# Attention probabilities: one tile for each head, normalised tiles copied by DMA into fp32r tiles, and the copies transposed

## The chip, the cores and the metric

The kernel runs on 1 core of one Trainium2 chip. The metric is the device time of one launch in microseconds. Three runs of the kernel before gave 1145.41, 1145.74 and 1146.05 us; the median, 1145.74 us, is the time before.

## The reference

One layer on 2048 tokens of 1024 channels, with 256 context tokens. All inputs are float32.

```python
h  = rms_norm(x)   * (1 + scale)   + shift      # scale, shift, gate from silu(c) @ w_ada + b_ada
hc = rms_norm(ctx) * (1 + scale_c) + shift_c
rq, rk, rv, rg, aq, ak, av, ag = project(h, w_in)   # one combined projection
# group A: bidirectional retention, 4 heads of 128, in chunks of 128 tokens
ret_x = group_norm(retention_fwd(rq, rk, rv) + retention_bwd(rq, rk, rv)) * gn_w * silu(rg)
# group B: windowed attention, 8 query heads of 64 over 2 key/value heads
def sink_softmax(logits, sink):
    m = maximum(max(logits, axis=-1), sink)
    p = exp(logits - m)
    return p / (sum(p, axis=-1) + exp(sink - m))
# for a block of 128 queries: 256 context keys and the block's own keys with both neighbour blocks (384)
p   = sink_softmax(concat([q @ k_ctx.T, where(valid, q @ k_window.T, -1e30)]), sink[head])
att = p[:, :256] @ v_ctx + p[:, 256:] @ v_window
x   = x + gate * (concat([ret_x, att * silu(ag)]) @ w_out)
out = rms_norm(x) * final_norm_w
```

## The kernel before

Up to about 680 us the kernel computes the modulated inputs, all projections (rq, rk, rv, rg, aq, ak, av, ag) and the retention states, and leaves them in DRAM scratch tensors. To keep float32's accuracy on TensorE each operand is split into a high part, rounded to the type fp32r, and a low part, the rest; a product is then three matmuls (high by high, high by low, low by high).

From there on it walks over the 16 blocks of 128 tokens, `b` = 0 to 15. A block has two half-steps, one for each key/value head `kv`, which serves four query heads. The string `STEPS[kv]` gives the order in which the pieces of a half-step are written down, and `FIRST` that of the very first half-step. The letters that matter here:

- `a0` to `a3` (`att_head`): the scores of one query head of the **next** half-step. Four matmuls fill a PSUM tile `S` (there is one such tile), a VectorE pass adds the mask, copies the scores into SBUF and takes the row maximum, a small VectorE operation makes the exponent's bias, and ScalarE takes the exponential of 640 scores and of one further column, the sink, and sums the row. At the first and last block 512 scores take the place of 640.
- `N0` to `N3` (`att_norm`): VectorE takes the reciprocal of the sum and GpSimd multiplies the head's row by it.
- `T0` to `T4` (`att_t`): TensorE transposes the probabilities of all four heads for one block of 128 keys into a PSUM tile `pt`; ScalarE rounds it to the high part, VectorE subtracts for the low part (tile `phl`, two buffers). The transposes of `T0` read all four heads, so they need the last `N`.
- `V0` to `V4` (`att_v`): the two matmuls of probabilities by values (PSUM tile `o`); `O` (`att_out`) brings the result to SBUF, gates it and splits it (`ma`).
- `o0` to `o7` (`piece`): three matmuls each of the output projection (PSUM tiles `pz`), on retention's part `mr` or attention's part `ma`. They depend on little and fill TensorE's queue between the others.
- `S`, `q`, `R`, `B`, `r`, `Y`, `U`: retention of the next block: scores, GpSimd's product `qd` of the queries with the decays (`q`, held behind the latest `N`), the matmuls `y` (`R`), the statistics, the normalisation of `sd` on ScalarE (`r`), its transposes `yt` and their gating `gr` with the split `mr` (`Y`), and the state update `st` on VectorE (`U`). `f` and `F`: final norm and store of the block before.

The probabilities of a half-step stand in one tile `p` of 128 x 4 x 641 float32 with two buffers; GpSimd writes the four sink columns into it. Loads and stores of this part are issued by one queue, SP's, in the order of the program: a load whose buffer is still in use holds up what stands behind it. A scheduler places the written operations on the engines by its own estimate of their times, so an engine's order is not exactly that of `STEPS`; each engine then works through its own list in order.

```python
PB[(b, kv)] = (C2["pool"].tile([P, 4, 641], F32, tag="pb", ...), ...)
pool.tensor_copy(PB[(b, kv)][0][:, :, n], sink8[:, 4 * kv : 4 * kv + 4])
pe.transpose(ppt[:, j], pb[:, j, kt * P : (kt + 1) * P], ident)
```

Elsewhere in the program, in the projection stage, four 128 x 512 tiles and one 128 x 256 tile of values are already copied from SBUF to SBUF by DMA into fp32r tiles (`vrx<-vt`, `vrc<-vtc`, line 539) and transposed there against the fp32r identity `identr` (line 546).

Of the kernel before, what the change touches and what calls it, by code (L numbers as in the profile page):

```python
# [39 lines left out]
def tile_hymba(  # L40
# [175 lines left out]
    def behind(i):  # L216
        return tc.issue_after(i.ins) if i else nullcontext()
# [516 lines left out]
    def att_head(b, kv, j):  # L734
# [8 lines left out]
        if j == 0:  # L743
            PB[(b, kv)] = (
                C2["pool"].tile([P, 4, 641], F32, tag="pb", name=f"p{b}_{kv}"),
                C2["pool"].tile([P, 3, 4], F32, tag="m4", name=f"m4{b}_{kv}"),
            )
            pool.tensor_copy(PB[(b, kv)][0][:, :, n], sink8[:, 4 * kv : 4 * kv + 4])
        pb, m4 = PB[(b, kv)]
        psc = pS.tile([P, 1024], F32, tag="S", name=f"S{b}_{h}")  # L750
        for hl in range(2):
# [5 lines left out]
        PE["S"] = i  # L757
        dve.tensor_tensor_reduce(  # L758
            out=pb[:, j, 0:n], in0=psc[:, o : o + n], in1=mk, op0=ALU.add, op1=ALU.max,
            scale=1.0, scalar=-3e38, accum_out=m4[:, 0, j : j + 1],  # L760
        )
        dve.tensor_scalar(  # L762
            m4[:, 1, j : j + 1], m4[:, 0, j : j + 1], -0.125, nsink[:, h : h + 1], op0=ALU.mult, op1=ALU.min
        )
        act.activation(  # L765
            pb[:, j, 0 : n + 1], pb[:, j, 0 : n + 1], AF.Exp, bias=m4[:, 1, j : j + 1], scale=0.125,
            accum_out=m4[:, 2, j : j + 1],
        )

    def att_norm(b, kv, j):  # L770
        n = len(window(b)[0]) * P + CTX
        pb, m4 = PB[(b, kv)]
        dve.reciprocal(m4[:, 2, j : j + 1], m4[:, 2, j : j + 1])  # L773
        PE["norm"] = pool.tensor_scalar(  # L774
            pb[:, j, 0:n], pb[:, j, 0:n], m4[:, 2, j : j + 1], 0.0, op0=ALU.mult, op1=ALU.add
        )

    BANKS = {"o": 1, "z": 2, "t": 3}
# [67 lines left out]
    def tables():  # L846
# [347 lines left out]
    pw = ctx.enter_context(tc.tile_pool(name="pw", bufs=1, space=PSUM, reuse_waits="tile"))  # L1194
    fw, vctx = C2["fw"], C2["vctx"]

    PO, PH = {}, {}

    def att_t(b, kv, kt):
        pb = PB[(b, kv)][0]  # L1200
        ppt = bank(f"pt{b}_{kv}_{kt}")
        for j in range(4):
            pe.transpose(ppt[:, j], pb[:, j, kt * P : (kt + 1) * P], ident)  # L1203
        phl = s2.tile([P, 2, 4, P], F32R, tag="phl", name=f"phl{b}_{kv}_{kt}", bufs=2)
        PE["phl"] = act.activation(phl[:, 0], ppt, AF.Copy)  # L1205
        PE["low"] = dve.tensor_tensor(phl[:, 1], ppt, phl[:, 0], op=ALU.subtract)  # L1206
        PH[kt] = phl
# [61 lines left out]
    def final_sum(b):  # L1269
        ss = s2.tile([P, 1], F32, tag="ss", name=f"ss{b}")  # L1270
        junk = s1.tile([P, D], F32, tag="junk", name=f"junk{b}", bufs=1)
        act.activation(junk, XB[b], AF.Square, scale=1.0 / 32, accum_out=ss)
# [7 lines left out]
    def last(b):  # L1280

        xb = XB[b]
        ss = s2.tile([P, 2], F32, tag="sl", name="sl")
        junk = s1.tile([P, D], F32, tag="junk", name="junkl", bufs=1)
        rz = s2.tile([P, 1], F32, tag="rz", name="rzl")
# [173 lines left out]
```

## Time and profile before

| | |
|---|---|
| median of 3 runs | 1145.74 us |
| the profiled execution | 1146.56 us, of which the span from first to last instruction 1144.8 us |
| mean granted TensorE clock | 0.995 |
| busy share of the span | TensorE 98%, VectorE 69%, ScalarE 41%, GpSimd 29% |

The profile of one execution lists, for every engine, instructions with their start and duration, and what ended the idle time before them. `PE` is TensorE's matmul unit, `PEld` its weight loads, which run beside the matmuls; `DVE` is VectorE, `ACT` ScalarE, `POOL` GpSimd, `SPq` the queue that issues DMAs. `L1203` is line 1203 of the program. In the projection stage and in the block loop the same profile can be asked for stretches (busy time of each engine between two times), for a timeline, for groups of instructions by line, for waits, and for the DMAs with the time from their issue to their landing. The block loop repeats itself almost exactly: the first transposes of block 6 start at 851.70 us, those of block 7 at 880.53 us, a period of 28.83 us.

### The profile page before, as it was taken

The numbers are of one execution on the slowest core, as the hardware profiler recorded it, in microseconds if no ns is written. First come the engines' busy times: TensorE is split into PE (matmuls) and PEld (weight loads), VectorE is DVE, ScalarE is ACT, GpSimd is POOL, SyncE is SP. The second block draws the span as 40 slices with busy tenths as digits, with TensorE's granted clock in tenths as the row PEclk, the third lists the DMA queues.
The fourth block names the chain that finished last, engine by engine and source line by source line (L and its number), as shares of the span: only waits on it lengthen the run. The fifth ranks groups of instructions, "written<-read, shape, count | busy, mean of one in ns | idle before, by whom it ended". The sixth has DMA issues, their size and how long they took to land.

```text
span 1144.8 us, 18064 instructions
## 1 busy us (share of the span) xinstructions
PE 1126.0 (98%) x6317; PEld 971.5 (85%) x6318; DVE 786.0 (69%) x1900; ACT 474.1 (41%) x1032; POOL 327.6 (29%) x459
## 2 busy tenths in 40 slices
PE   9999999999999999999999999999999999999997
PEld 5887879989888889998888877888888888888885
DVE  7973994665674555656566457777777777777774
ACT  4344512332443002322111156555555566666553
POOL 0000020100111100002014344555555555555553
PEclk9999999999999999999999999999999999999999
DMA  9948893374675533543356275444444444444310
GB/s 334 337 148 262 292 284 127 116 264 138 196 231 170 148 105 88 177 125 107 115 170 205 88 195 208 133 132 130 132 130 132 133 133 132 134 134 134 98 56 37
DMA packets 140113, 183.43 MB, mean 160 GB/s; under 512 B 11251, under 2 KB 103155, under 8 KB 139894
## 3 DMA queue, kind: packets, MB, share of 16 engines
q1 hardware_dynamic: 124948, 174.64, 48.6%
q10 hardware_dynamic: 15074, 7.64, 2.2%
q8 instruction: 50, 0.82, 0.3%
q14 instruction: 41, 0.34, 0.1%
HBM read 130.19 MB, written 50.86 MB: 158 GB/s over the span
## 4 chain that ended last, share of the span: by engine, by line
PE 81%; DVE 7%; issue 5%; ACT 3%; DMA 2%; POOL 1%; POOLq 0%; DVEq 0%; ACTq 0%
PE pz L1253 14%; PE rk L340 7%; PE rv L353 7%; PE ag L340 6%; PE o L1216 6%; PE pt L1203 5%; PE aq L340 5%; PE rg L340 4%; PE rq L340 4%; PE S L752 4%; PE S L756 2%; PE av L340 2%; PE ak L340 2%; PE u L469 2%; DVE wss L214 1%
## 5 line engine op out<-in xcount | busy, mean ns | idle before, releaser
L765 ACT ACTIVATE p<-p,m 128x641 f32<-128x641 f32 (+1 forms) x128 | 104.6, 817 | 60.3 <-DVE m L762 59.9
L774 POOL TENSOR_SCALAR p<-p,m 128x640 f32<-128x640 f32 (+1 forms) x128 | 101.8, 795 | 89.3 <-DVE m L773 82.5
L1205 ACT ACTIVATE phl<-pt 128x512 fp32r<-128x512 f32 x156 | 92.6, 595 | 78.3 <-PE pt L1203 76.3
L1206 DVE TENSOR_TENSOR phl<-pt,phl 128x512 fp32r<-128x512 f32 x156 | 106.3, 683 | 24.1 <-ACT phl L1205 23.4
L758 DVE CUSTOM_DVE_ANT_0 p<-S,msk 128x640 f32<-128x640 f32 (+1 forms) x128 | 102.4, 800 | 13.3 <-PE S L756 6.6
L1253 PE MATMUL pz<-wg1h,ma 128*128 128x512 f32 x256 | 106.1, 420 | 0.1
L1253 PE MATMUL pz<-wg0h,mr 128*128 128x512 f32 x256 | 103.6, 409 | 0.6 <-DVE mr L115 0.6
L1203 PE MATMUL pt<-ident,p 128*128 128x128 f32 x624 | 93.2, 272 | 0.6 <-DVE glast L1186 0.6
L1203 PEld LDWEIGHTS pt<-ident,p 128*128 128x128 f32 x624 | 75.2, 140 | 9.2 <-ACT first L833 0.8
L752 PE MATMUL S<-kwin,aq 128*128 128x384 f32 (+1 forms) x256 | 79.4, 332 | 0.6 <-DVE m L758 0.5
L445 ACT ACTIVATE vw<-v,wdec 128x128 fp32r<-128x128 f32 x128 | 43.7, 393 | 84.9 <-DVE v L458 84.9
L756 PE MATMUL S<-kctx,aq 128*128 128x256 f32 x256 | 71.1, 280 | 0.0
L1216 PE MATMUL o<-phl,vwin 128*128 128x512 f32 x184 | 62.2, 416 | 1.3 <-DVE phl L1206 0.8
L1253 PEld LDWEIGHTS pz<-wg0h,mr 128*128 128x128 f32 x256 | 48.1, 188 | 9.3 <-DVE mr L115 0.9
L1253 PEld LDWEIGHTS pz<-wg1h,ma 128*128 128x128 f32 x256 | 48.1, 188 | 7.9 <-POOL ma L1231 0.5
L752 PEld LDWEIGHTS S<-kwin,aq 128*128 128x128 f32 x256 | 48.0, 188 | 7.6 <-DVE m L758 2.3
L756 PEld LDWEIGHTS S<-kctx,aq 128*128 128x128 f32 x256 | 48.2, 188 | 5.2
L1253 PE MATMUL pz<-wg0l,mr 128*128 128x512 f32 x128 | 50.6, 395 | 0.0
L1253 PE MATMUL pz<-wg1l,ma 128*128 128x512 f32 x128 | 50.3, 393 | 0.0
L447 DVE SCALAR_TENSOR_TENSOR vw<-v,wdec,vw 128x128 fp32r<-128x128 f32 x128 | 40.6, 362 | 6.8 <-ACT vw L445 6.7
L1227 DVE TENSOR_TENSOR mf<-o,ob 64x256 f32<-64x256 f32 x64 | 26.7, 417 | 24.4 <-ACT ob L1224 23.7
L1216 PE MATMUL o<-phl,vctx 128*128 128x512 f32 x128 | 41.6, 404 | 0.2 <-DVE phl L1206 0.2
(425 smaller groups left out, 3001.7 us busy)
## 6 DMA issues: line engine op xcount, KB each, us to landing
wss<-in_wss SPq DMA_DIRECT2D x32, 512.0 KB, 6.6
qkv<-d_qkv SPq DMA_DIRECT2D x15, 768.0 KB, 4.8
aq<-d_aq SPq DMA_DIRECT2D x64, 128.0 KB, 3.9
xb<-in_xn SPq DMA_DIRECT2D x16, 512.0 KB, 3.8
out<-xb SPq DMA_DIRECT2D x31, 256.0 KB, 5.0
st<-d_st SPq DMA_DIRECT2D x15, 512.0 KB, 8.4
d_g<-g ACTq DMA_DIRECT2D x28, 256.0 KB, 2.9
x<-in_xt SPq DMA_DIRECT2D x12, 512.0 KB, 5.2
```

The costliest lines, as they stand in the source:

```text
L340: pe.matmul(ps, w[:, a, k, c0 : c0 + P], ht[b][:, k, :], start=(k == 0 and i == 0), stop=(k == NK - 1 and i == 2),)
L353: pe.matmul(ps, ht[a][:, k, t * P : (t + 1) * P], w[:, b, k, :], start=(k == 0 and i == 0), stop=(k == NK - 1 and i == 2),)
L752: i = pe.matmul(psc[:, o:512].rearrange("p (s t) -> p s t", t=P), AQ[b][:, h, :], C2["kwin"][:, kv, hl, ksel], start=(hl == 0), stop=(hl = ...
L756: pe.matmul(psc[:, 512:768], AQ[b][:, h, :], C2["kctx"][:, kv, hl], start=(hl == 0), stop=(hl == 1))
L758: dve.tensor_tensor_reduce(out=pb[:, j, 0:n], in0=psc[:, o : o + n], in1=mk, op0=ALU.add, op1=ALU.max, scale=1.0, scalar=-3e38, accum_out= ...
L765: act.activation(pb[:, j, 0 : n + 1], pb[:, j, 0 : n + 1], AF.Exp, bias=m4[:, 1, j : j + 1], scale=0.125, accum_out=m4[:, 2, j : j + 1],)
L774: PE["norm"] = pool.tensor_scalar(pb[:, j, 0:n], pb[:, j, 0:n], m4[:, 2, j : j + 1], 0.0, op0=ALU.mult, op1=ALU.add)
L1203: pe.transpose(ppt[:, j], pb[:, j, kt * P : (kt + 1) * P], ident)
L1205: PE["phl"] = act.activation(phl[:, 0], ppt, AF.Copy)
L1206: PE["low"] = dve.tensor_tensor(phl[:, 1], ppt, phl[:, 0], op=ALU.subtract)
L1216: pe.matmul(PO[kv], vt, PH[kt][:, hl], start=(kt == 0 and hl == 0), stop=(kt == nkt - 1 and hl == 1))
L1253: pe.matmul(PZ[n2], m[:, a, k % RH, :], WG[k // 4][c][:, k % 4, s], start=(k == 0 and i == 0), stop=(k == NK - 1 and i == 2),)
```

## The change

Each query head gets a tile of its own, 128 x 641 float32, from a tag with three buffers. The sink column is copied into it by VectorE, head by head, behind the pass that writes the scores, in place of GpSimd's one copy for four heads. After GpSimd has normalised a head, SP issues a DMA that copies its 128 x 640 probabilities from SBUF to SBUF into a tile `pr` of type fp32r with room for four heads (two buffers). The transposes read `pr` against `identr` and write the PSUM tile as fp32r. In `STEPS`, `o1` is moved ahead of `T0` in both half-steps.

Around it: the final norm's weights `fw` are loaded when the block loop's pools are opened, and not with the tables before; `glast`, the last gate's tile, takes a buffer of the tag `aq`, whose second buffer so far held the queries of block 1; the two scratch outputs `junk` are bf16.

```diff
 STEPS = (
-    "a0 o0 O T0 r0 o1 a1 N0 T1 r1 o2 V0 U a2 N1 T2 o3 Y V1 o4 a3 N2 T3 o5 V2 q o6 T4 N3 o7 V3 S f V4",
-    "a0 o0 O T0 o1 a1 N0 T1 R F0 F1 V0 a2 N1 T2 B V1 o2 a3 N2 T3 o3 V2 o4 T4 r2 N3 o5 V3 o6 V4 o7",
+    "a0 o0 O o1 T0 r0 a1 N0 T1 r1 o2 V0 U a2 N1 T2 o3 Y V1 o4 a3 N2 T3 o5 V2 q o6 T4 N3 o7 V3 S f V4",
+    "a0 o0 O o1 T0 a1 N0 T1 R F0 F1 V0 a2 N1 T2 B V1 o2 a3 N2 T3 o3 V2 o4 T4 r2 N3 o5 V3 o6 V4 o7",
 )
...
         if j == 0:
             PB[(b, kv)] = (
-                C2["pool"].tile([P, 4, 641], F32, tag="pb", name=f"p{b}_{kv}"),
+                C2["pool"].tile([P, 4, 640], F32R, tag="pr", name=f"pr{b}_{kv}"),
                 C2["pool"].tile([P, 3, 4], F32, tag="m4", name=f"m4{b}_{kv}"),
+                [C2["pool"].tile([P, 641], F32, tag="pb", name=f"p{b}_{kv}_{i}", bufs=3) for i in range(4)],
             )
-            pool.tensor_copy(PB[(b, kv)][0][:, :, n], sink8[:, 4 * kv : 4 * kv + 4])
...
-        dve.tensor_tensor_reduce(
-            out=pb[:, j, 0:n], in0=psc[:, o : o + n], in1=mk, op0=ALU.add, op1=ALU.max,
+        i = dve.tensor_tensor_reduce(
+            out=pb[:, 0:n], in0=psc[:, o : o + n], in1=mk, op0=ALU.add, op1=ALU.max,
             scale=1.0, scalar=-3e38, accum_out=m4[:, 0, j : j + 1],
         )
+        with behind(i):
+            dve.tensor_copy(pb[:, n : n + 1], sink8[:, h : h + 1])
...
         PE["norm"] = pool.tensor_scalar(
-            pb[:, j, 0:n], pb[:, j, 0:n], m4[:, 2, j : j + 1], 0.0, op0=ALU.mult, op1=ALU.add
+            pb[:, 0:n], pb[:, 0:n], m4[:, 2, j : j + 1], 0.0, op0=ALU.mult, op1=ALU.add
         )
+
+        nc.sync.dma_start(pr_[:, j, 0:n].bitcast(F32), pb[:, 0:n])
...
-        fw = new("fw", [P, D])
-        nc.sync.dma_start(fw, fnw)
...
-        new("glast", [P, 2, GT])
+        C2["glast"] = c2.tile([P, 2, GT], F32, tag="aq", name="glast")
...
-    fw, vctx = C2["fw"], C2["vctx"]
+    vctx = C2["vctx"]
+    fw = s2.tile([P, D], F32, name="fw", bufs=1)
+    nc.sync.dma_start(fw, fnw)
...
-            pe.transpose(ppt[:, j], pb[:, j, kt * P : (kt + 1) * P], ident)
+            pe.transpose(ppt[:, j].bitcast(F32R), pb[:, j, kt * P : (kt + 1) * P], identr)
```

How the engines' lists change is shown at three places. The first is TensorE's list in block 6, second half-step, from the scores `S_0` of the next half-step's first head on. `pt_1_0` are the transposes of `T0`, `pt_1_1` those of `T1`; x4 is four instructions, one for each head in turn. Before:

```order
L752 MATMUL S_0_8559<-kwin,aq_8204 128x384
L756 MATMUL S_0_8559<-kctx,aq_8204 128x256
L752 MATMUL S_0_8559<-kwin,aq_8204 128x384
L756 MATMUL S_0_8559<-kctx,aq_8204 128x256
L1253 MATMUL pz_0_8567<-wg0h,mr_8472 128x512
L1253 MATMUL pz_0_8567<-wg0l,mr_8472 128x512
L1253 MATMUL pz_0_8567<-wg0h,mr_8472 128x512
L1203 MATMUL pt_1_0_8580<-ident,p_1_8376 128x128 x4
L1253 MATMUL pz_0_8567<-wg0h,mr_8472 128x512
```

And now, from the last rows of the projection on:

```order
L1259 MATMUL pz_0_8725<-wg0h,mr_8623 128x512
L1209 MATMUL pt_1_0_8741<-identr,pr_1_8519 128x128 x3
L753 MATMUL S_1_8749<-kwin,aq_8336 128x384
L757 MATMUL S_1_8749<-kctx,aq_8336 128x256
L753 MATMUL S_1_8749<-kwin,aq_8336 128x384
L757 MATMUL S_1_8749<-kctx,aq_8336 128x256
L1209 MATMUL pt_1_1_8761<-identr,pr_1_8519 128x128 x3
L1209 MATMUL pt_1_0_8741<-identr,pr_1_8519 128x128
L1209 MATMUL pt_1_1_8761<-identr,pr_1_8519 128x128
L813 MATMUL y_8769<-st_8225,qd_8657 128x128
```

Six projection matmuls stand ahead of `T0` now and not three, and the fourth head's transpose stands behind the scores `S_1` and three transposes of `T1`. In the first half-step it is alike: six projection matmuls, three transposes, the scores of the second head, the fourth transpose, then `T1` without anything between.

The second is ScalarE's list in block 6, first half-step, from `ob` (the copy that `O` makes) on; `p` with `m` is the exponential of a head, `phl` the rounding of a group of transposes, `sd` retention's normalisation, four heads in two pairs. Before:

```order
L1224 ACTIVATE ob_1_8390<-o_1_8284 64x512
L1205 ACTIVATE phl_0_0_8403<-pt_0_0_8398 128x512
L765 ACTIVATE p_1_8376,m_1_8377<-p_1_8376,m_1_8377 128x641
L833 ACTIVATE sd_8162<-sd_8162,ra_8315 128x128 x2
L1205 ACTIVATE phl_0_1_8426<-pt_0_1_8421 128x512
```

And now:

```order
L1230 ACTIVATE ob_1_8537<-o_1_8422 64x512
L768 ACTIVATE p_1_0_8521,m_1_8520<-p_1_0_8521,m_1_8520 128x641
L1211 ACTIVATE phl_0_0_8553<-pt_0_0_8548 128x512
L839 ACTIVATE sd_8293<-sd_8293,ra_8455 128x128 x2
L1211 ACTIVATE phl_0_1_8575<-pt_0_1_8570 128x512
```

The exponential and the rounding of the first group have changed places; the second rounding still stands behind both and behind a pair of `sd`.

The third is SP's list where the block loop begins: `aq` are the queries of block 1, `gr`, `ga`, `xb` the gates and inputs of block 0. Before:

```order
L684 DMA vwin_6830<-d_v 128x256
L715 DMA aq_6503<-d_aq 32x8x128 x3
L701 DMA gr_6409<-d_g 128x512
L730 DMA ga_6411<-d_g 128x256
L731 DMA xb_6412<-in_xn 128x1024
```

And now:

```order
L782 DMA pr_1_6288<-p_1_2_6292 128x512
L715 DMA aq_6443<-d_aq 32x8x128 x2
L782 DMA pr_1_6288<-p_1_3_6293 128x512
L1201 DMA fw<-in_fnw 128x1024
L701 DMA gr_6431<-d_g 128x512
L730 DMA ga_6433<-d_g 128x256
L731 DMA xb_6434<-in_xn 128x1024
```

The loads of block 0 stand behind the copy of the last head of block 0 and behind `fw`; the other half of `aq` follows after the loads of block 1's `qkv` and `st`.

More of the change, by code (lines that the diff above doesn't have):

```diff
@@ L765, in att_head @@
         act.activation(
-            pb[:, j, 0 : n + 1], pb[:, j, 0 : n + 1], AF.Exp, bias=m4[:, 1, j : j + 1], scale=0.125,
+            pb[:, 0 : n + 1], pb[:, 0 : n + 1], AF.Exp, bias=m4[:, 1, j : j + 1], scale=0.125,
             accum_out=m4[:, 2, j : j + 1],
@@ L1270, in final_sum @@
         ss = s2.tile([P, 1], F32, tag="ss", name=f"ss{b}")
-        junk = s1.tile([P, D], F32, tag="junk", name=f"junk{b}", bufs=1)
+        junk = s1.tile([P, D], BF16, tag="junk", name=f"junk{b}", bufs=1)
         act.activation(junk, XB[b], AF.Square, scale=1.0 / 32, accum_out=ss)
@@ L1283, in last @@
         ss = s2.tile([P, 2], F32, tag="sl", name="sl")
-        junk = s1.tile([P, D], F32, tag="junk", name="junkl", bufs=1)
+        junk = s1.tile([P, D], BF16, tag="junk", name="junkl", bufs=1)
         rz = s2.tile([P, 1], F32, tag="rz", name="rzl")
```

6 lines of the change are left out of this document (4 added, 2 removed).

## The prediction

> **What bounds the kernel now.** I read the shares of the span first, then the chain that ended last, then the block loop by stretches, then TensorE's waits there.
>
> ```profile
> span 1144.8 us, 18064 instructions
> PE 1126.0 (98%) x6317; PEld 971.5 (85%) x6318; DVE 786.0 (69%) x1900; ACT 474.1 (41%) x1032; POOL 327.6 (29%) x459
> PE 81%; DVE 7%; issue 5%; ACT 3%; DMA 2%; POOL 1%; POOLq 0%; DVEq 0%; ACTq 0%
> 680.00:715.00 35.00, 32.00 (x187) 26.37 (x186) 24.38 (x72) 21.45 (x42) 13.39 (x20) 1.00 0.62 207
> 715.00:1100.00 385.00, 385.00 (x2359) 342.35 (x2357) 305.84 (x890) 229.34 (x468) 207.44 (x296) 1.00 0.43 127
> PE y L807 <- DVE m L773: 1.0, 1, 1.0
> ```
>
> The columns of the two stretches are length, then busy time of TensorE, its weight loads, VectorE, ScalarE and GpSimd, then clock, DMA share and GB/s. Between 715 and 1100 us TensorE is busy for 385.0 of 385.0 us: nothing holds it up, so any instruction made shorter there shortens the kernel, and any wait that arises lengthens it. The last row is its longest wait in the whole block loop, 1.0 us, in the loop's first blocks. VectorE is busy for 305.84 of 385 us (79%).
>
> **What the change removes: time of the transposes.** The groups of four, as float32 in the loop and as fp32r where the kernel has them already:
>
> ```profile
> L1203 PE MATMUL pt<-ident,p 128*128 128x128 f32 x624 | 93.2, 272 | 0.6 <-DVE glast L1186 0.6
> 851.70 0.60 PE L1203 MATMUL pt<-ident,p 128*128 128x128 f32 x4
> 852.05 0.48 PE L1253 MATMUL pz<-wg1h,ma 128*128 128x512 f32 x1
> 852.36 0.39 PE L1253 MATMUL pz<-wg1l,ma 128*128 128x512 f32 x1
> 551.17 0.45 PE L546 MATMUL pvx<-identr,vrx 128*128 128x128 f32 x4
> 551.76 0.40 PE L340 MATMUL aq<-h0l,w_aaq 128*128 128x512 f32 x1
> ```
>
> From the group's start to the second matmul behind it pass 0.66 us (852.36 - 851.70) in float32 and 0.59 us (551.76 - 551.17) in fp32r: 0.07 us a group. 624 transposes are 156 groups, so **-10.9 us** if nothing else moves. A block has ten groups: -0.70 us of its period.
>
> **What it adds: a hop by DMA between the last `N` and `T0`.** Block 6, second half-step, on GpSimd and TensorE:
>
> ```profile
> 858.99 0.62 POOL L111 TENSOR_SCALAR mr<-gr 128x512 fp32r<-128x512 f32 x1 [0.49 <-DVE gr L1239]
> 859.69 1.31 POOL L1242 TENSOR_TENSOR mr<-gr,mr 128x512 fp32r<-128x512 f32 x1
> 860.97 0.80 POOL L774 TENSOR_SCALAR p<-p,m 128x640 f32<-128x640 f32 x1
> 861.74 2.54 POOL L792 TENSOR_TENSOR qd<-qkv,decq 128x512 f32<-128x512 f32 x2
> 864.25 0.81 POOL L774 TENSOR_SCALAR p<-p,m 128x640 f32<-128x640 f32 x1
> 864.16 0.34 PE L752 MATMUL S<-kwin,aq 128*128 128x384 f32 x1
> 864.75 0.40 PE L1253 MATMUL pz<-wg0h,mr 128*128 128x512 f32 x1
> 864.98 0.39 PE L1253 MATMUL pz<-wg0l,mr 128*128 128x512 f32 x1
> 865.45 0.60 PE L1203 MATMUL pt<-ident,p 128*128 128x128 f32 x4
> ```
>
> `N3` ends at 864.25 + 0.81 = 865.06 and `T0` starts at 865.45: it has 0.39 us to spare. GpSimd gets to `N3` late because it runs `mr`, `N2` and `qd` in one piece behind `gr`. In the new list the fourth head's transpose comes behind three more projection matmuls (0.23 us each by 864.75 and 864.98: 0.70), three transposes (3 x 0.07 = 0.22), four score matmuls (864.16 to 864.75: 0.59, and 0.08 for the change behind transposes, 852.36 - 852.05 less 0.23), and three transposes of `T1` (0.22): 865.45 + 1.81 = 867.26. So the list leaves 2.2 us for the hop. What it takes:
>
> ```profile
> vrx<-vt SPq DMA_DIRECT2D x4, 256.0 KB, 2.3
> vrc<-vtc SPq DMA_DIRECT2D x1, 128.0 KB, 2.1
> DMA to landing us min/median/max: 2.3/2.3/2.6
> out<-xb SPq DMA_DIRECT2D x31, 256.0 KB, 5.0
> ```
>
> These copies of 128 rows from SBUF to SBUF take 2.1 us for 128 KB and 2.3 for 256 KB from issue to landing; at 0.1 us per 64 KB, 320 KB take **2.4 us** (estimate). The bounds are 2.1 and the stores' 5.0 us, which stand behind a 768 KB load; I take the near row, since nothing large is issued ahead of this head's copy. Landing: 865.06 + 2.4 + 0.05 for SP to start = 867.5, already 0.2 us late. Two things widen it.
>
> TensorE itself arrives earlier: the five groups of the first half-step are shorter, 5 x 0.07 = 0.35 us, of which I give back 0.1 (the transposes `yt` are now mixed with other matmuls): 867.0.
>
> And `N3` moves later, through the first half-step:
>
> ```profile
> 848.63 0.81 POOL L774 TENSOR_SCALAR p<-p,m 128x640 f32<-128x640 f32 x1 [0.37 <-DVE m L773]
> 851.00 0.40 PE L1253 MATMUL pz<-wg1h,ma 128*128 128x512 f32 x1
> 852.33 0.60 ACT L1205 ACTIVATE phl<-pt 128x512 fp32r<-128x512 f32 x1 [1.80 <-PE pt L1203]
> 852.83 0.83 ACT L765 ACTIVATE p<-p,m 128x641 f32<-128x641 f32 x1
> 853.66 0.86 ACT L833 ACTIVATE sd<-sd,ra 128x128 f32<-128x128 f32 x2
> 854.43 0.58 ACT L1205 ACTIVATE phl<-pt 128x512 fp32r<-128x512 f32 x1
> 855.65 1.13 DVE L841 SCALAR_TENSOR_TENSOR st<-st,gC,st 128x128 f32<-128x128 f32 x4
> 856.69 0.82 DVE L758 CUSTOM_DVE_ANT_0 p<-S,msk 128x640 f32<-128x640 f32 x1
> 858.22 0.68 DVE L1239 TENSOR_TENSOR gr<-yt,gr 128x512 f32<-128x512 f32 x1
> ```
>
> There the hop itself fits: `N3` ends at 849.44 and the fourth transpose comes at 851.00 + 6 x 0.23 + 0.22 + 0.67 = 853.3, 3.9 us later. But the first group is complete only then, and no longer at 852.05. ScalarE now does the exponential first (852.85 to 853.7), the first rounding (to 854.2, 0.5 from start to next start), the `sd` pair (0.77, by 853.66 and 854.43), and starts the second rounding at 854.95, 0.5 us later than before. VectorE's `st` update follows it, then the third head's pass, then `gr`: all 0.5 us later, and 0.1 more for the new sink copy in between. `gr` feeds `mr`, and with `N2` and `qd` behind it `N3` ends near 865.65. Copy landed: 865.65 + 2.45 = 868.1, TensorE there at 867.0: it **stands still for 1.1 us in each block**, and what is queued behind, `T1`'s last transpose and the twelve `y`, waits with it. In blocks 1 to 14: 14 x 1.1 = **+15.4 us**; the 0.1 above: **+1.4**.
>
> By the Trainium skill's page "DMA: Bandwidth & Descriptors", section "Anatomy of one DMA — SWDGE (gpsimd) path", a DMA costs about 2.0 us plus bytes at 436 GB/s; for 320 KB that is 2.75 us, an estimate of mine for copies that here come from SP and not from GpSimd. The rows of `vrx` and `vrc` lie below it (2.6 by the rule for 256 KB, 2.3 measured); by the rule the sum would be 14 x 0.35 = 4.9 us larger.
>
> **The sink columns.** GpSimd loses 32 copies, VectorE gets 128:
>
> ```profile
> L748 POOL COPY p<-sink 128x4 f32<-128x4 f32 x32 | 6.1, 194 | 2.2 <-PE pt L1203 2.2
> L762 DVE TENSOR_SCALAR m<-m,nsink 128x1 f32<-128x1 f32 x128 | 26.2, 205 | 0.3
> ```
>
> The neighbour of one column takes 0.205 us, part of it overlapped with the next instruction; between nothing and 0.2 I take 0.1 us, 0.8 us a block of VectorE's 28.83. VectorE's slack (21%) hides it except on the chain above, where it is counted. The three head buffers cost nothing while the copies land: a buffer is written again three heads later, and heads are some 3 us apart. The `junk` tiles keep their instructions.
>
> **Where the loop begins.** In the new list `fw` (512 KB) and all loads of block 0 stand on SP behind the copy of block 0's last head:
>
> ```profile
> 681.78 0.38 SPq L701 DMA_DIRECT2D gr<-d_g  x1
> 684.75 0.69 POOL L774 TENSOR_SCALAR p<-p,m 128x512 f32<-128x512 f32 x1 [2.94 <-DVE m L773]
> 690.47 0.50 PE L1253 MATMUL pz<-wg0h,mr 128*128 128x512 f32 x1 [0.56 <-DVE mr L115]
> gr<-d_g SPq DMA_DIRECT2D x16, 256.0 KB, 5.0
> ```
>
> That head is normalised at 685.44, so `gr` is issued at about 686.4 in place of 681.78 and lands, at its median of 5.0, at 691.4; gating and splitting (0.68 and 0.42) let the projection start at 692.5 in place of 690.47. TensorE has nothing else in its list there: 2.0 us. Block 1's scores come later too, the second half of its queries being behind the loads of blocks 0 and 1, so all of block 0's projection is used up before block 1's first transposes, and its four `S` then follow each other at VectorE's pace: 0.82 for a pass behind the 0.59 of its matmuls, some 0.5 us idle each: 2.0 us. **+4 us**, between 0 (loads land in time) and 8.
>
> **The sum**: -10.9 + 15.4 + 1.4 + 4 = +9.9 us on the profiled execution's own 1146.56 us (span 1144.8 and 1.8 around it), 1156.5. That execution was 0.8 above the median of 1145.74, against which I forecast **1155.6 us**; by its own bounds (a wait of 0.7 to 1.6 us a block, the beginning 2 to 6) 1148 to 1165.
>
> **The rivals.** (1) The hop is hidden: TensorE waits 0.2 us or less a block. For it: only 0.2 us is missing before the two shifts, and `vrc` lands in 2.1. Against it: TensorE's own gain of 0.35 is certain to come off the margin. Sum -10.9 + 2.8 + 1.4 + 2 = -4.7: 1141; with no wait at all 1136.
>
> (2) The first half-step waits as well. `xb`'s load waits on SP until the store of the same buffer lands, 5.0 us by the row above, and in the new list the copy of the third head stands behind that load. From the point where the landing passes the end of `N2`, that copy is issued late and queues behind 512 KB; I price it at 1 us more in each of 14 blocks: 1170. Against it: even `N3`, the head behind it, has 3.9 us there.
>
> (3) Gain and waits cancel: a wait of 0.4 us (5.6) with 1.4 and 4 against 10.9, 1146.
>
> (4) The transposes don't get faster in the loop, say because the weight loads beside them set the pace: the same waits less TensorE's earlier arrival, 0.75 x 14 + 1.4 + 4, +16: 1162.
>
> **Chances.** Forecast 0.52, rival 1 0.26, rival 2 0.11, rival 3 0.08, rival 4 0.03. 0.2% (2.3 us) is about what a measurement of this kernel can tell from no change. Faster 0.26, within it 0.08, slower 0.52 + 0.11 + 0.03 = 0.66. The range takes in most of rival 1 and the lower part of rival 2: 1138 to 1168.
>
> **What would show it.** Right: TensorE's busy time falls by about 10 us, and the waits list a new row of `pt` on the DMA of `pr`, 14 times near 1 us, always at a second half-step's first group; `gr` to `N3` starts 0.5 us later against the block's first scores; the projection at the loop's start begins near 692.5. Wrong: a `pt` row that waits under 0.3 us, or waits in the first half-step, or a copy that lands in under 2.2 or over 3 us.

## The result, and the profile after

The changed kernel takes **1180.69 us** (median of four runs, 1180.29 to 1181.46), the kernel before 1145.89 on the same chip: ratio 1.0304, 95% interval 1.0286 to 1.0322, 34.8 us slower. I had forecast 1155.6, with a range up to 1168. The direction was right, the size was not.

The page of the changed kernel, then its stretches (columns as in the prediction), then the longest waits of TensorE for the copies between 740 and 1120 us (total, times, longest):

```profile
span 1178.7 us, 18728 instructions
PE 22%; POOL 7%; DMA 6%; DVE 4%; issue 2%; ACT 1%; SPq 0%; POOLq 0%; DVEq 0%
L1209 PE MATMUL pt<-identr,pr 128*128 128x128 f32 x624 | 76.3, 241 | 22.2 <-DMA pr<-p 20.0
pr<-p SPq DMA_DIRECT2D x112, 320.0 KB, 3.2
```
```profile
680.00:715.00 35.00, 30.39 (x156) 23.81 (x154) 17.77 (x54) 15.23 (x28) 10.55 (x14) 0.90 0.75 250
715.00:740.00 25.00, 18.13 (x99) 15.36 (x99) 16.62 (x50) 11.66 (x25) 11.10 (x14) 0.80 0.39 135
740.00:1100.00 360.00, 341.96 (x2092) 296.12 (x2090) 281.09 (x896) 208.10 (x420) 180.63 (x240) 1.00 0.64 215
```
```profile
PE pt L1209 <- DMA pr<-p: 18.0, 18, 1.3
```

The chain that ended last was TensorE for 81% before. Now the profile follows it back to 678.6 us only, so its shares add up to less than half of the span; within it TensorE has about half, and GpSimd and the copies come next. In the loop TensorE is busy for 341.96 of 360 us, where it had been busy throughout. Between 715 and 740 us, where nothing was missing before, it works 18.13 of 25 us at a granted clock of 0.80.

Where the 34 us lie is read from one recurring point, the first scores (`a0`) of a block's first half-step:

| first scores of | before | after | behind by |
|---|---|---|---|
| block 2 | 735.08 | 750.53 | 15.5 |
| block 3 | 763.91 | 781.33 | 17.4 |
| block 13 | 1052.25 | 1081.67 | 29.4 |
| block 14 | 1081.08 | 1111.66 | 30.6 |
| block 15 | 1109.78 | 1143.35 | 33.6 |
| end of the span | 1144.8 | 1178.7 | 33.9 |

So 15.5 us are lost **before block 2**, about 1.2 us in each block after it, 3.0 us in block 14 alone. Beside the wait below, TensorE also waits for copies in three first half-steps between blocks 3 and 12, up to 0.35 us each time. (In the expectations below, "block 2's second half-step starts at 750.5" means the first row of this table; the point belongs to the first half-step, the name is a slip of mine.)

The wait in the loop is the one forecast. Block 6, second half-step of the changed kernel, on GpSimd, SP and TensorE:

```profile
883.58 2.54 POOL L798 TENSOR_TENSOR qd<-qkv,decq 128x512 f32<-128x512 f32 x2
886.10 0.80 POOL L778 TENSOR_SCALAR p<-p,m 128x640 f32<-128x640 f32 x1
```
```profile
886.93 0.50 SPq L782 DMA_DIRECT2D pr<-p  x1
887.48 1.74 SPq L715 DMA_DIRECT2D aq<-d_aq  x3
```
```profile
885.28 0.34 PE L753 MATMUL S<-kwin,aq 128*128 128x384 f32 x1
887.24 0.37 PE L1209 MATMUL pt<-identr,pr 128*128 128x128 f32 x3
888.11 0.37 PE L1209 MATMUL pt<-identr,pr 128*128 128x128 f32 x3
889.78 0.36 PE L1209 MATMUL pt<-identr,pr 128*128 128x128 f32 x2 [1.29 <-DMA pr<-p]
```

`N3` ends at 886.90, the copy is issued at once, and the fourth head's transpose starts at 889.78, **2.88 us** behind `N3`. TensorE had reached it at 888.3; from the transpose's start before the wait to its start after it pass 1.54 us in place of 0.07, so the wait costs 1.47.

At the beginning the block's fourth set of scores waits for VectorE, which has block 0's projection and final norm first:

```profile
712.87 0.69 DVE L1264 TENSOR_TENSOR xb<-pz,xb 128x512 f32<-128x512 f32 x1 [2.94 <-PE pz L1259]
717.13 1.41 DVE L1283 SCALAR_TENSOR_TENSOR xb<-xb,rz,fw 128x512 f32<-128x512 f32 x2 [2.20 <-DMA st<-d_st]
718.46 0.82 DVE L759 CUSTOM_DVE_ANT_0 p<-S,msk 128x640 f32<-128x640 f32 x1
```
```profile
719.43 0.66 PE L753 MATMUL S<-kwin,aq 128*128 128x384 f32 x1 [5.03 <-DVE p L764]
```

(The name `st` in the second row is the profile's attribution: the norm needs `rz`, which GpSimd ends at 717.10.) The pass at 718.46 empties the one tile `S`; until then TensorE stands for 5.03 us, and the matmul behind the stop takes 0.66 us in place of 0.34.

### The profile page after: what moved, and what is told of

Read it like the earlier page. It is cut to its first block, busy times and chain, and to the rows that moved or that the text cites. A ratio compares the mean times of both kernels' runs of the same rounds, so it can differ in the third digit from the quotient of the medians.

```text
span 1178.7 us, 18728 instructions
## 1 busy us (share of the span) xinstructions
PE 1132.1 (96%) x6317; PEld 966.0 (82%) x6318; DVE 796.4 (68%) x2028; ACT 476.7 (40%) x1032; POOL 323.3 (27%) x427
## 5 line engine op out<-in xcount | busy, mean ns | idle before, releaser
L1259 PE MATMUL pz<-wg0h,mr 128*128 128x512 f32 x256 | 100.3, 407 | 1.2 <-DVE mr L115 1.0
L1259 PE MATMUL pz<-wg1h,ma 128*128 128x512 f32 x256 | 100.1, 409 | 0.1
L1209 PEld LDWEIGHTS pt<-identr,pr 128*128 128x128 f32 x624 | 70.1, 141 | 34.5 <-DMA pr<-p 23.0
L1209 PE MATMUL pt<-identr,pr 128*128 128x128 f32 x624 | 76.3, 241 | 22.2 <-DMA pr<-p 20.0
L753 PE MATMUL S<-kwin,aq 128*128 128x384 f32 (+1 forms) x256 | 84.2, 349 | 8.0 <-DVE p L764 5.0
L1222 PE MATMUL o<-phl,vwin 128*128 128x512 f32 x184 | 70.7, 445 | 2.0 <-DVE phl L1212 1.5
L1222 PEld LDWEIGHTS o<-phl,vwin 128*128 128x128 f32 x184 | 33.0, 193 | 12.5 <-ACT phl L1211 4.5
```

The lines of the kernel that those rows point to most:

```text
L753: i = pe.matmul(psc[:, o:512].rearrange("p (s t) -> p s t", t=P), AQ[b][:, h, :], C2["kwin"][:, kv, hl, ksel], start=(hl == 0), stop=(hl = ...
L1209: pe.transpose(ppt[:, j].bitcast(F32R), pb[:, j, kt * P : (kt + 1) * P], identr)
L1222: pe.matmul(PO[kv], vt, PH[kt][:, hl], start=(kt == 0 and hl == 0), stop=(kt == nkt - 1 and hl == 1))
L1259: pe.matmul(PZ[n2], m[:, a, k % RH, :], WG[k // 4][c][:, k % 4, s], start=(k == 0 and i == 0), stop=(k == NK - 1 and i == 2),)
```

## The experiments

All runs in one table. "Block 2" is the start of its first scores; "a block" is the mean period from block 3 to block 13, from the same starts. The ratio is against the kernel before on the same chip; its median was 1145.6 to 1146.8 us.

| run | us | ratio (95%) | block 2 | a block |
|---|---|---|---|---|
| before | 1145.9 | | 735.1 | 28.83 |
| changed | 1180.7 | 1.0304 (1.0286-1.0322) | 750.5 | 30.03 |
| e1 | 1147.4 | 1.0009 (1.0000-1.0019) | 734.9 | 28.83 |
| e2 | 1178.9 | 1.0286 (1.0263-1.0310) | 751.7 | 30.10 |
| e3 | 1172.0 | 1.0225 (1.0203-1.0247) | 752.0 | 29.15 |
| e4 | 1140.9 | 0.9964 (0.9953-0.9975) | 735.1 | 28.40 |
| e5 | 1177.9 | 1.0288 (1.0266-1.0310) | 750.7 | 30.25 |
| e6 | 1233.8 | 1.0770 (1.0750-1.0790) | 752.0 | 33.97 |
| e7 | 1228.5 | 1.0715 (1.0697-1.0733) | 750.0 | 34.17 |
| e8 | 1180.8 | 1.0307 (1.0288-1.0326) | 756.8 | 29.94 |
| e9 | 1182.7 | 1.0314 (1.0291-1.0336) | 750.7 | 30.30 |
| e10 | 1154.4 | 1.0072 (1.0045-1.0099) | 752.1 | 28.42 |
| e11 | 1154.7 | 1.0072 (1.0053-1.0091) | 740.0 | 29.15 |
| e12 | 1178.3 | 1.0290 (1.0260-1.0321) | 751.2 | 30.25 |
| e13 | 1151.2 | 1.0044 (1.0031-1.0056) | 735.3 | 29.11 |
| e14 | 1168.9 | 1.0194 (1.0178-1.0209) | 741.6 | 30.08 |
| e15 | 1156.4 | 1.0086 (1.0072-1.0101) | 740.2 | 29.21 |
| e16 | 1152.2 | 1.0050 (1.0035-1.0064) | 740.8 | 29.04 |
| e17 | 1149.9 | 1.0024 (1.0012-1.0035) | 737.4 | 29.22 |
| e18 | 1137.5 | 0.9925 (0.9910-0.9939) | 736.0 | 28.10 |

The profiles differ ahead of the loop, too: block 0's first scores start between 668.5 and 674.9 us, so a few microseconds in the column "block 2" say nothing. From block 0's first scores to block 2's pass 64.6 us before, 80.6 in the changed kernel, 65.2 in e1, 77.4 in e2, 66.7 in e4, 76.4 in e5, 78.6 in e9, 80.4 in e10, 69.8 in e11 and in e14.

**Is the beginning lost to block 1's queries? (e1, e2)** In the trace the first scores of block 1 come at 701.7 us where they had come at 681.6 (the 688.8 of the expectation is its second head). Comparing the lists, I found an error of mine in the third list shown above: in the kernel before the three loads `aq` there are block 2's. Block 1's four stand earlier, ahead of `kwin`:

```
L715 DMA aq_6421<-d_aq 32x8x128 x4
L679 DMA kwin<-d_k 64x2x128 x4
L684 DMA vwin_6501<-d_v 128x256
L684 DMA vwin_6830<-d_v 128x256
L715 DMA aq_6503<-d_aq 32x8x128 x3
```

Since `glast` takes a buffer of `aq`, block 1's queries now wait for block 0's last scores. That looked like the cause.

```diff
 e1 (before)  -        new("glast", [P, 2, GT])
              +        C2["glast"] = c2.tile([P, 2, GT], F32, tag="aq", name="glast")
 e2 (changed) -        C2["glast"] = c2.tile([P, 2, GT], F32, tag="aq", name="glast")
              +    two tiles of tag "pb" take its place
```

> The kernel before with one part of the change alone: the last gate's tile takes a buffer of the tag of the queries. Theory Q (block 1's queries find no buffer until block 0's last scores are done, so block 1's first scores come some 12 us later and TensorE runs out of work): block 1's first scores move from 688.8 us to 700 or later, and the time rises by 9 to 16 us, to 1155-1162. Rival S (the loop's beginning is lost on SP's queue, behind the copies and the load of fw, neither of which is here): 1145-1149, first scores before 693 us.

> The changed kernel with the last gate in two of the three head buffers instead of a buffer of the queries; copies, fw and all else stay. Q: block 1's queries are loaded as early as before, the start of block 2's second half-step comes back from 750.5 us to 735-738, and the time falls by 12 to 15 us, to 1165-1169. S: SP's queue is as full as in the changed kernel, 1177-1181.

Theory Q falls. In e1 block 1's first scores come at 696.7, 15 us later than before, and the time rises by 1.0 us (between 0 and 2.2). e2 gives 1.8 us back, within its interval; it is the weaker test, since its gate holds two of the three head buffers at first. The next runs add the clearest: e4 keeps the late queries and loses nothing.

**What is the wait in the loop, and what do the copies cost in all? (e3, e4)**

```diff
 e3 - o5 V2 q o6 T4 N3 o7 V3
    + o5 V2 o6 T4 N3 q o7 V3
 e4 - pb[:, 0:n], pb[:, 0:n], m4[...]        (GpSimd, in place)
    - nc.sync.dma_start(pr_[:, j, 0:n].bitcast(F32), pb[:, 0:n])
    + pr_[:, j, 0:n], pb[:, 0:n], m4[...]    (GpSimd, rounded)
```

> The changed kernel with q written behind N3 in the first half-step: on GpSimd the product qd changes places with the fourth head's normalisation, and nothing else moves. Theory W (the wait at the second half-step's first transposes is the copy of a head that GpSimd normalises late): N3 ends 2.5 us earlier, the copy lands 1.0 us before TensorE gets there, the wait of 1.47 us a block goes: 14 x 1.47 = 20.6 less, 1160 (1157-1164). Rival L (the copy is held up by the loads and the third head's copy that were issued ahead of it, and lands at the same time whenever it is issued): 1175-1181. Rival M (the wait moves to the products y, which need qd, now 0.8 us later): 1165-1172, with waits at the matmuls y.

> The changed kernel without the DMA: GpSimd writes the normalised row, rounded, straight into the fp32r tile, so the low part of the probabilities is left out (zero, though still computed and multiplied). W: every wait of the transposes on a copy goes, 14 x 1.47 = 20.6 and some 2 more in the last block; the beginning's loss stays: 1156-1160. Rival: the beginning is lost to the copies as well: 1143-1148. Rival: the changed order on TensorE costs by itself, the waits only show it: 1165 or more.

Without the copy the kernel is 0.36% **faster** than before (0.25 to 0.47), and the beginning is back too (735.1): all 40 us between e4 and the changed kernel come with the copies. My expectation that the beginning's loss would stay was wrong. In e3 the period fell by 0.88 us, not by the whole 1.47: `N3` ends 2.5 us earlier, but its copy takes longer. (The profiled execution took 1167.8 us, the three others 1171 to 1173.4.)

```profile
909.93 1.59 POOL L778 TENSOR_SCALAR p<-p,m 128x640 f32<-128x640 f32 x2
```
```profile
910.77 0.50 SPq L782 DMA_DIRECT2D pr<-p  x1
911.36 0.54 SPq L715 DMA_DIRECT2D aq<-d_aq  x1
912.00 0.50 SPq L782 DMA_DIRECT2D pr<-p  x1
```
```profile
915.90 0.37 PE L1209 MATMUL pt<-identr,pr 128*128 128x128 f32 x2 [0.26 <-DMA pr<-p]
```

`N3` ends at 911.52, a load on SP holds the issue until 912.00, and the third head's copy is only 1.2 us old: from `N3` to the transpose pass 4.38 us, 1.50 more than in the changed kernel. Rival L holds in part. The time lies in rival M's range, but its sign does not show: between 740 and 1120 us the matmuls `y` wait for `qd` once, 0.9 us.

**Bytes or a fixed time? (e8)**

```diff
-        nc.sync.dma_start(pr_[:, j, 0:n].bitcast(F32), pb[:, 0:n])
+        w = n if b < 2 else P
+        nc.sync.dma_start(pr_[:, j, 0:w].bitcast(F32), pb[:, 0:w])
```

> The changed kernel, in which from block 2 on each copy moves the first 128 columns alone, 64 KB in place of 320; the other columns of the transposed tile keep older probabilities. Theory T (the copy's time is its bytes beside the loads'): it lands in 2.2 us or less in place of 2.85, the wait falls from 1.47 to 0.7-0.8, 14 x 0.7 = 10 less, 1169-1172. Rival F (it is a fixed time from issue to landing): 1177-1181. The beginning is as in the changed kernel under both.

```profile
892.50 0.80 POOL L778 TENSOR_SCALAR p<-p,m 128x640 f32<-128x640 f32 x1
```
```profile
893.58 0.37 PE L1210 MATMUL pt<-identr,pr 128*128 128x128 f32 x3
895.19 0.28 PE L1210 MATMUL pt<-identr,pr 128*128 128x128 f32 x1 [1.25 <-DMA pr<-p]
895.30 0.41 PE L753 MATMUL S<-kwin,aq 128*128 128x384 f32 x1
```

The time lies in F's range, the trace shows T: from `N3`'s end (893.30) to the transpose pass 1.89 us in place of 2.88, a whole microsecond less for a fifth of the bytes. The wait is still there because the scheduler, which knows the size, now lists the fourth transpose ahead of the scores `S_1`: TensorE gets to it 0.5 us after `N3` and not 1.4. What the copy gained, the list gave away.

**Another queue for the copies? (e6, e7)** `nc.sync` becomes `nc.scalar` (e6) or `nc.gpsimd` (e7).

> The changed kernel with the copies issued by ScalarE's queue instead of SP's: same copies, same bytes, none behind a load. O: VectorE's list then has the passes in the order of the program, and the beginning comes back to within 4 us of the kernel before; if the wait of 1.47 us a block stays (the copy's own time), 1163-1168; if queueing on SP was part of it, down to 1150. Rival C: the bytes are the same, 1175 or more. Rival A (ScalarE waits in its list for GpSimd's normalisation before it can issue, and its exponentials and roundings wait behind): over 1170 with new waits on ScalarE.

> The changed kernel with the copies issued by GpSimd, right behind its own normalisation, so that no queue waits for anything. O: the beginning as in the run with ScalarE's queue. In the loop GpSimd pays for the issue what no row here shows; between 0.05 and 1 us a copy: at the low end 1160-1168, at the high end four copies a half-step lengthen the chain mr, N2, qd, N3 by 1 to 2 us and the wait of 1.47 with it, 1175-1190.

Both cost about 4 us more in every block. GpSimd's part in e7, then TensorE's and ScalarE's waits in e6 (740 to 1100 us):

```profile
883.94 0.80 POOL L778 TENSOR_SCALAR p<-p,m 128x640 f32<-128x640 f32 x1
885.03 0.62 POOL L782 DMA_DIRECT2D pr<-p  x1 [0.30 <-POOL p L778]
```
```profile
ACT p L768 <- DVE m L765: 70.8, 62, 3.8
PE pt L1209 <- DMA pr<-p: 28.7, 27, 2.5
```

On GpSimd an issue takes 0.92 us with the wait before it, on the engine whose chain was late already. From ScalarE's queue TensorE's waits for copies grow from 18.0 to 28.7 us, and ScalarE's own waits ahead of the exponentials from 39.1 to 70.8. In both runs the waits come with a slower clock: from 750 to 1100 us the mean granted clock is 0.95 in e6 and 0.96 in e7, 1.00 in the changed kernel (how a stop lowers it stands in the last section). Rival A's time came, its details are not shown. SP was the best of the three.

**The beginning: an order, or the copies? (e5, e9, e10)** The list puts block 0's sum and norm ahead of a pass (the rows at 712.87). e5 forbids that for one instruction; e9 gives the changed kernel the four lists of e4 up to block 2, by a table of numbers from which each instruction is tied behind the one before (SP's list stays the scheduler's); e10 gives e4 the changed kernel's lists.

```diff
 e5  +            with behind(PE["pass103"] if b == 0 else None):
                      dve.tensor_tensor(XB[b][:, s], PZ[n2], XB[b][:, s], op=ALU.add)
 e9, e10
     +        if t == 4:
     +            for e, table in ORDER.items():   # PE, DVE, Activation, Pool
     ...
     +                for a, c in zip(order, order[1:]):
     +                    tc.add_manual_dep(mine[c], mine[a].name, ...)
```

> The changed kernel with one constraint: VectorE's addition of block 0's projection into xb must stand behind the pass over the fourth head's scores of block 1. Theory O (the beginning's loss is an order: VectorE's list has block 0's sum and final norm ahead of that pass, the one score tile stays full, TensorE stands for 5.0 us at 714 and runs at a granted clock of 0.80 until 740): the 5 us stop goes and part of the slow clock with it, block 2's second half-step starts at 739-743 in place of 750.5, 1168-1173 us. Rival C (the copies themselves land late among the loads, whatever the order): a stop of the same size appears at another place, 1177-1181.

> The changed kernel, copies and all, with the lists of TensorE, VectorE, ScalarE and GpSimd up to the start of block 2 put in the order that the run without copies has there (a table of numbers); SP's list and everything from block 2 on stay the scheduler's. Theory O (the beginning's 15 us are an order: the scheduler reckons with late copies and puts other work ahead): block 2's second half-step starts at 735-740 in place of 750.5, 1164-1170 us. Rival C (the copies' own time among the loads): the order changes nothing or makes it worse, 1177 or more.

> The mirror of it: the kernel without copies (GpSimd writes the rounded row into the fp32r tile, the low part of the probabilities is left out) with the four lists up to the start of block 2 in the order of the changed kernel. O: the beginning's loss is there without a single copy, block 2's second half-step starts at 747-751 in place of 735.1, 1152-1157 us. C: 1140-1143, as without copies.

e10 loses 13.5 us against e4 without one copy: the order is enough to make the loss. e9 has the good order and loses as much: the copies are enough, too. In e9 the stop is only renamed (waits between 700 and 755 us; the second row is a pass that waits until a head tile's copy has landed):

```profile
PE pt L1296 <- DMA pr<-p: 9.3, 6, 3.1
DVE p L846 <- DMA pr<-p: 2.4, 1, 2.4
```

So the order alone is not to blame: with the good order the wait for copies takes its place. That the scheduler chose its order because it reckoned with that wait is likely, not shown. In e5 the stop of 5.03 us is gone and shorter ones, up to 1.1 us, stand in its place; 4.2 of the 16.0 us come back by the count from block 0, and its time is not clearly different from the changed kernel's.

In three runs the three head buffers can be read as a part of it. The pass over the fourth head of block 1 stands until the copy of the first head has landed, whose buffer it takes: 4.71 us in e7 and 2.39 in e9 (below), 4.25 in e6.

```profile
714.79 0.82 DVE L759 CUSTOM_DVE_ANT_0 p<-S,msk 128x640 f32<-128x640 f32 x1 [4.71 <-DMA pr<-p]
711.42 0.82 DVE L846 CUSTOM_DVE_ANT_0 p<-S,msk 128x640 f32<-128x640 f32 x1 [2.39 <-DMA pr<-p]
```

Since e6 and e7 issue no copy from SP and their block 2 is as late (752.0 and 750.0), the loss does not need loads that stand behind copies on SP's queue.

**What fp32r and the order of the steps are worth (e11, e13, e18)** e11 is e4 with float32 tiles and transposes; e13 is the kernel before with the new `STEPS`; e18 is e4 with the old `STEPS`.

> The run without copies with the tile of four heads and its transposes in float32 (so the low part of the probabilities is there again): what fp32r saves in the transposes, with nothing else in the way. By my 0.07 us a group: 10.9 over the run without copies, 1151-1152. Rival: by TensorE's shares in the loop, 0.28 to 0.43 us a block of 28.8, only 4 to 7 us: 1145-1148.

> The kernel before with the new order of the steps alone (o1 ahead of T0 in both half-steps). In its list for TensorE the two matmuls o of V0 in the first half-step no longer stand in a pair: scores of the third head come between them, as in the changed kernel. Theory I (that order costs TensorE 0.31 us a block, seen in the shares of o and S with and without copies): 14 x 0.31 = 4.3 more, 1150-1151. Rival: the order is free, and the 0.31 us come from the single-head tiles or the copies of the sink on VectorE: 1145-1147.

> The run without copies (rounded probabilities, their low part left out) in the order of the steps of the kernel before. Theory I: 0.31 us a block less than without copies and o1 ahead, 14 x 0.31 = 4.3 of 1140.9: 1136-1137, which is my 10.9 us of faster transposes off the kernel before. Rival: the order costs nothing where the transposes are fp32r: 1140-1142.

TensorE's time in one block, from each matmul's start to the next one's, added up by the tile it writes (mean of blocks 3 to 12):

```
        before    e13    e11     e4  changed
pz       11.81  11.63  11.60  11.62  11.57
o         4.95   5.07   5.16   5.19   5.24
S         4.70   4.97   4.94   4.84   4.94
pt        3.62   3.63   3.62   2.92   3.07
y, s, yt  3.76   3.82   3.83   3.83   3.75
wait      0      0      0      0      1.47
sum      28.83  29.11  29.15  28.40  30.03
```

Between e11 and e4 only the transposes' type differs: 3.62 to 2.92, **0.070 us a group**, as forecast. Between before and e13 only the order: **+0.28 us a block**. Its place, first before, then e13 (block 6, first half-step):

```profile
854.32 0.39 PE L1253 MATMUL pz<-wg1h,ma 128*128 128x512 f32 x1
854.55 0.62 PE L1216 MATMUL o<-phl,vwin 128*128 128x512 f32 x2
855.01 0.34 PE L752 MATMUL S<-kwin,aq 128*128 128x384 f32 x1
855.60 0.60 PE L1203 MATMUL pt<-ident,p 128*128 128x128 f32 x4
```
```profile
855.54 0.40 PE L1253 MATMUL pz<-wg1h,ma 128*128 128x512 f32 x1
855.94 0.50 PE L1216 MATMUL o<-phl,vwin 128*128 128x512 f32 x1
856.27 0.41 PE L752 MATMUL S<-kwin,aq 128*128 128x384 f32 x1
856.84 0.50 PE L1216 MATMUL o<-phl,vwin 128*128 128x512 f32 x1
857.30 0.60 PE L1203 MATMUL pt<-ident,p 128*128 128x128 f32 x4
```

The pair `o` is split by scores, and from the last `pz` to the next transposes pass 1.76 us in place of 1.28; part of it comes back elsewhere (`pz` is 0.2 lower). Theory I holds, and e18 shows it once more (28.40 to 28.10 a block). e18, 9.4 us below before, is what the faster transposes are worth (with the tiles of single heads and their sink copies) when neither copy nor order takes it back; it is no solution, since it lacks the low part of the probabilities.

**A version with copies that costs nothing? (e12, e14 to e17)** e12 has e9's kind of lists, and in the loop `M`, the low part of `mr`, behind `N3`. e14 copies only from block 2 on; blocks 0 and 1 stay float32. e15 joins e14 with `M` and puts the loads of `gr` and `xb` behind the fourth copy; e16 moves `o1` back behind `T0`; e17 keeps block 0's final norm behind a pass.

```diff
 e12 - o6 T4 N3 o7 V3 S f V4        e15 - ... q o6 T4 N3 o7 / ... r2 N3 o5
     + o6 T4 N3 M q o7 V3 S f V4        + ... o6 T4 N3 M q g o7 / ... r2 N3 x o5
 e14 + HOP = 2     (b < HOP: F32 tile written by GpSimd, transposed against ident, no DMA)
 e16 - "a0 o0 O o1 T0 r0 a1 ...", "a0 o0 O o1 T0 a1 ..."
     + "a0 o0 O T0 r0 o1 a1 ...", "a0 o0 O T0 o1 a1 ..."
 e17 + with behind(PE["pass201"] if b == 0 else None):   (final norm of block 0)
```

> The changed kernel with both repairs: the lists up to block 2 as without copies, and in the loop GpSimd's order mr (high part), N2, N3, mr (low part), qd, so that the last two copies leave some 3.3 and 2.3 us earlier than in the changed kernel, 1.4 us apart. O and W together: no loss at the beginning, no wait of the transposes in second half-steps, 1141-1146. If copies close together slow each other as in the run with q behind N3: waits of 0.4 us a half-step stay, 1148-1155. C: 1160 or more.

> The changed kernel, in which blocks 0 and 1 go without the copy (GpSimd writes their normalised rows into a float32 tile, and they are transposed as float32); from block 2 on as changed. If the copies of these two blocks are behind the beginning's loss: block 2's second half-step starts at 735-741 in place of 750.5, the loop is as in the changed kernel (30.0 us a block): 1165-1172. If not: 1177-1182.

> The same, and in the loop: GpSimd's order mr (high part), N2, N3, mr (low part), qd; the load of gr and of xb stand behind the fourth head's copy on SP. N3 ends 3 us earlier than in the changed kernel, no load ahead of its copy: at 2.85 us of hop the transposes' waits go, 28.4-28.6 us a block, 1142-1150. If copies 1.4 us apart still hold each other up: waits of 0.4 to 1 us a block stay, 1150-1160.

> The same with the order of the steps of the kernel before (o1 behind T0): TensorE comes to the transposes 0.7 us earlier, with 0.8 us to spare if the hop is 2.85. Theory I: 0.31 us a block less than the run with o1 ahead, 1138-1146. If the hop is longer than 3.6 us: waits come back, not faster than that run.

> The run with copies in time and o1 behind T0, and one more constraint: block 0's final norm on VectorE stands behind the second head's pass of block 2. The stop of 2.7 us at 723 and the slow clock behind it go: block 2's second half-step starts at 736-738 in place of 740.8, 3 to 4.5 us less, 1147-1149: no faster than the kernel before. If the loop's two late copies (2 us each) also go, 1143-1146.

In e12 `N3` is 3 us earlier and the wait stays: my own edit had put a load ahead of the copy. `gr`'s buffer is read by `mr`'s low part, which I had moved behind `N3`:

```profile
885.46 0.80 POOL L865 TENSOR_SCALAR p<-p,m 128x640 f32<-128x640 f32 x1 [0.58 <-DVE m L864]
886.22 1.28 POOL L1340 TENSOR_TENSOR mr<-gr,mr 128x512 fp32r<-128x512 f32 x1
```
```profile
887.53 0.33 SPq L788 DMA_DIRECT2D gr<-d_g  x1
887.94 0.50 SPq L869 DMA_DIRECT2D pr<-p  x1
```

The copy is issued 1.7 us after `N3`. In e14 sixteen of 128 copies are gone, and 11.8 us with them; what is left of the beginning's loss (741.6 against 735.1) float32 blocks without any copy have too (e11, 740.0). With the loads out of the way (e16), TensorE's waits for copies between 740 and 1120 us are

```profile
PE pt L1219 <- DMA pr<-p: 4.5, 4, 2.1
```

and most blocks take 28.5 us. The four late copies that remain, up to 2.1 us each, and in e15 and e16 the 5 us still lost before block 2 (740.2 and 740.8) keep these runs from their lower bounds; what makes the four late is not settled. No version with copies beats the kernel before: e17 is nearest, 0.24% slower.

## Why the prediction was wrong, step by step

- **The transposes, -10.9.** The price was right (0.070 us a group in e4 against e11), and rival 4 falls. In the changed kernel it arrives, too: beside the wait, block 6's ten groups take 2.93 us (2.92 in e4). The 3.07 of the table holds short waits in some first half-steps.
- **The wait of `T0`, 14 x 1.1.** Place, cause and number of times were right, the size was not: 1.47 us. The mis-sized term is the hop. Counted from the half-step's first scores, my sum has `N3` end 1.74 us behind them (865.65 against 864.16 less 0.25) and TensorE arrive 3.1 behind them; measured are 1.62 and 3.0. I had 2.45 us from `N3` to landing; 2.88 us pass from `N3` to the transpose. My figure holds for a copy with nothing behind it: in block 14, where no load follows, the transpose starts 2.46 us behind `N3`, which ends at 1127.06:

```profile
1126.24 0.82 POOL L778 TENSOR_SCALAR p<-p,m 128x640 f32<-128x640 f32 x1
1129.52 0.28 PE L1209 MATMUL pt<-identr,pr 128*128 128x128 f32 x1 [1.96 <-DMA pr<-p]
```

  In the twelve blocks before it three `aq` loads are issued right behind the copy, and the same stretch takes 2.84 to 2.91 us. That the loads cause the difference fits, but no run moved them alone. It is 14 x 0.37 = 5 us of the miss. The rule of the Trainium skill's page "DMA: Bandwidth & Descriptors", section "Anatomy of one DMA — SWDGE (gpsimd) path", which I had set aside, gives an estimate of 2.75 us. That is nearer to the 2.88, and above the 2.46 of block 14.
- **"0.1 more for `yt`", 1.4.** The transposes `yt` cost nothing more. What the new order of the steps costs is 0.28 us a block, 3.9 us, and it lies in the scores between the two `o`. I had read that list only for what stands ahead of `T0`. So a block loses 1.47 + 0.28 + 0.1 (the short waits) - 0.70 = 1.15 us by these terms; 1.20 is measured.
- **The beginning, +4, "between 0 and 8".** This is the step that failed: 15.5 us. Its first part did not come: the projection begins at 690.86, not 692.5, since `gr` is issued at 685.24 and is there 4.4 us later. Its real cause, the copies of blocks 0 and 1, I had dismissed in one sentence, "The three head buffers cost nothing while the copies land", and in the view that only what SP loads is late there. The sentence counts heads 3 us apart; in e9 the first three passes of block 1 start within 4.6 us, and the first buffer is free again only 8.1 us behind the first pass. In blocks 0 and 1 the hop has little cover: each head goes through pass, exponential, normalisation and copy, and TensorE soon waits for it. e14 shows that 11.8 us go with the copies of these two blocks, e9 that the order of the run without copies does not undo the loss. How much of it is the three head buffers and how much the hop itself stays open: a fourth buffer was not tried.
- **The clock.** I had no term for it. The stop at 714 us halves it from 718.0 to 728.2 us:

```profile
718.00:728.24 10.24, 7.22 (x27) 6.40 (x28) 5.64 (x21) 5.30 (x13) 2.40 (x3) 0.50 0.25 96
```

  TensorE is busy there for 7.22 us at 0.50; at the full clock the same work would take half, so some 3.6 us are lost (an estimate from this row) beside the stop's 5.0.
- **The last block**, 3.0 us, was not in the sum: a wait of 2.1 us at 1127 us (1.96 of them idle), and behind it 3.41 us at a clock of 0.50.
- **The rivals.** Transposes in the first half-step (rival 2) wait up to 0.5 us in some blocks, not 1; rival 1 is what e16 comes near to, with four edits that the change lacks.
- **The signs I had named.** The new row is there where I said, but TensorE's busy time did not fall by 10 us: it rose from 1126.0 to 1132.1, the slow stretches included. Waits in the first half-step and copies that take over 3 us (3.2 in the median from issue to landing) were my signs of being wrong, and both came.

## What to carry to other kernels

Price a new hop where its cover is thinnest, at the beginning of a loop, not in its steady state: here 16 of 128 copies cost 12 us. A stop of the bottleneck engine is to be charged with the clock that follows it. And where a scheduler places the work, a shorter wait may only move the consumer ahead: compare the lists, not the times alone.

## What the runs showed of the hardware

- In these traces the granted clock is 1.00 or 0.50 and changes only at steps of 3.41 us. A drop goes with TensorE's idle time within one such step. The stop of 1.96 us at 1127 us lies in one (first row, 1.49 of 3.41 us busy) and the next runs at 0.50 (second row); so does e17's stop of 2.09 us (third row), with the same effect. In e16 a stop of 2.05 us at 886 us is divided between two steps, 0.78 and 1.38 us idle (last two rows), and the clock stays at 1.00. So it does behind the stops of about 1.5 us in 14 blocks. Steps with 1.6 to 1.8 us idle went either way (1.62 in e6 from 735.02, slow behind it; 1.82 in e2 from 1128.08, not). The stop of 5.0 us brought 10.24 us at 0.50.

```profile
1127.60:1131.01 3.41, 1.49 (x14) 1.49 (x15) 1.89 (x6) 1.49 (x4) 1.59 (x3) 1.00 0.45 173
1131.01:1134.42 3.41, 3.41 (x19) 3.41 (x18) 2.40 (x9) 1.15 (x3) 1.38 (x2) 0.50 0.14 50
881.99:885.40 3.41, 1.25 (x8) 0.82 (x7) 1.42 (x6) 0.00 (x0) 1.13 (x2) 1.00 0.92 287
883.59:887.01 3.42, 2.64 (x15) 1.99 (x13) 2.19 (x7) 0.59 (x1) 0.45 (x2) 1.00 0.88 300
887.01:890.42 3.41, 2.03 (x13) 1.90 (x14) 0.95 (x2) 1.71 (x5) 0.83 (x2) 1.00 0.62 209
```

  The Trainium skill's page "TensorE: Matmul & The Clock Gate", section "What's actually happening", has the clock halved after an idle window of about 3.4 us. The 3.41 us agree; the window did not have to be idle throughout, 1.92 and 2.16 us of it were enough.

- A copy of 320 KB from SBUF to SBUF was used 2.88 us after the instruction before it ended where three loads of 128 KB were issued behind it, 2.46 us where none was; one of 64 KB 1.89 us after it; one issued 1.2 us behind another of 320 KB, with a load between, 4.38 us after it.
- A DMA that GpSimd issues takes 0.62 us of GpSimd and a wait of 0.30 ahead of it; SP took 0.50 for the same copy.
